# Channel blocks 4 to 7 of the normed rows in a pool of their own, 448 bytes behind the place of the weights modulo 512, in a decoder trunk on one core

## The chip, the cores and the metric

The kernel runs on one core of one Trainium2 chip. The metric is the device time of one execution in microseconds, as the median of several runs. A profile is taken of one execution apart from these.

## The reference, cut to what matters

Two layers over 512 tokens with 1024 channels, each a feed-forward part (ffn1), a mixing part (mix) and a second feed-forward part (ffn2). Everything is float32.

```python
D_MODEL, SEQ, DEPTH, D_FF = 1024, 512, 2, 2816

def swiglu(x, w_in, w_out):
    gate, up = jnp.split(x @ w_in, 2, axis=-1)
    return (jax.nn.silu(gate) * up) @ w_out

for l in range(DEPTH):
    mod = (c_act @ w_ada[l] + b_ada[l]).reshape(B, N_MOD, D_MODEL)
    sh1, sc1, gt1, sh2, sc2, gt2, sh3, sc3, gt3 = [mod[:, i, None, :] for i in range(N_MOD)]
    hn = rms_norm(h, g_ffn1[l]) * (1.0 + sc1) + sh1
    h = h + 0.5 * (1.0 + gt1) * swiglu(hn, w_ffn1_in[l], w_ffn1_out[l])
    hn = rms_norm(h, g_mix[l]) * (1.0 + sc2) + sh2
    proj = hn @ w_mix_in[l]
    ...
    mixed = jnp.concatenate([y_att, y_rwkv, y_conv], axis=-1) @ w_mix_out[l]
    h = h + (1.0 + gt2) * mixed
    hn = rms_norm(h, g_ffn2[l]) * (1.0 + sc3) + sh3
    h = h + 0.5 * (1.0 + gt3) * swiglu(hn, w_ffn2_in[l], w_ffn2_out[l])
```

## The kernel before

Activations are held transposed, 128 channels on the partitions by 512 tokens, so that the 1024 channels are eight blocks. A weight tile is 128 x 8 x 128 (4096 bytes in each partition). Each operand of a large product is kept as two tiles of a reduced-precision float type, a high part (names ending in H) and the rest (ending in L). `split` (L92 to L95) makes them: ACT casts the high part (L94), DVE subtracts it for the low one (L95). `mm3` (L86 to L91) forms a product from three matmuls: wH by xH, wH by xL and wL by xH. In a matmul the weights w are loaded (PEld in the profile) and the rows x move past them.

The tiles that the change touches come from one pool, `hnp` (L66), of 16 tiles of 128 x 512 (2048 bytes in each partition), all with one tag. `norm` (L202) takes eight pairs hnH, hnL from it, one pair for each channel block, and `apply` (L231) writes them in token halves of 256 columns: DVE forms hn_t (L235), ACT writes hnH (L236), DVE hnL (L237). `begin` (L1070) takes the first eight pairs, for the first layer. `mix` takes its results y0 to y5 and two yr through `pair` (L522), since the normed rows are done with by then; y0 to y3 are attention's four blocks, yr the recurrent part's two, y4 and y5 the convolution's.

Three users read them as moving rows:

- `projector` (L252) multiplies the eight blocks by 8 x 3 matmuls for each weight tile. Its first three tiles go in two halves of 256 columns, the others 512 wide. It does the projections of mix and the first tiles of each feed-forward part.
- `pair_in` (L378), in the feed-forward parts. It forms a block of 2 x 2 products (two halves of the channels, two halves of the tokens) with seven products instead of eight. Each product is a `prod` (L365 to L372) of 24 matmuls 256 wide. In order: ps_f from P1, ps_d from B11 (blocks 0 to 3, low half), the previous pair's last product on T4 (`flush`), ps_d from P2, ps_g from B21 (blocks 4 to 7, low half), ps_d from T3, ps_f from B22 (blocks 4 to 7, high half). P1, P2, T3 and T4 are sums of normed rows, formed once per feed-forward part. 34 pairs run in all.
- the product of w_mix_out with the y tiles, 512 wide for most tiles and 256 wide for the last.

The sums P1 to T4 are the `com` tiles. They lie in the pool of the feed-forward part behind a filling tile of GAP = 448 bytes (L300), and a second one of 64 bytes (L302) brings the tiles behind it back. In the built program the weight tiles wH and wL begin at 384 bytes modulo 512 in each partition, all hn and y tiles at 384, the act tiles (inputs of w_out) at 384, and the com tiles at 320. The last two tiles of each w_out product are 256 wide and use com's slots for their weights, so that there the weights lie at 320 and the rows at 384.

SP issues the weight loads (tile wraw; `load_w`, L243), POOL issues those of the conditioning weights (wada) and adding DMAs for the summed weights. The order on each engine is set by a scheduler when the program is built: it takes what is ready by its own model, so that another layout of the pools can change the order in which instructions stand on an engine.

Of the kernel before, what the change touches and what calls it, by code (L numbers as in the profile page):

```python
# [8 lines left out]
F32 = mybir.dt.float32  # L9
F32R = mybir.dt.float32r  # L10
# [7 lines left out]
P = 128  # L18
D = 1024
T = 512  # L20
L = 2
KD = D // P
# [10 lines left out]
GAP = 448  # L33
# [25 lines left out]
def trunk_kernel(ctx, tc, ins, out, layers=L, phases=("ffn1", "mix", "ffn2")):  # L59
# [3 lines left out]
    small_ = ctx.enter_context(tc.tile_pool(name="small", bufs=2))  # L63
    hp_ = ctx.enter_context(tc.tile_pool(name="hres", bufs=1))
    wp = ctx.enter_context(tc.tile_pool(name="wp", bufs=3))
    hnp = ctx.enter_context(tc.tile_pool(name="hnp", bufs=2 * KD))  # L66
    sp = ctx.enter_context(tc.tile_pool(name="sp", bufs=2))
    ps = ctx.enter_context(tc.tile_pool(name="ps", bufs=4, space=PSUM))
    dram = ctx.enter_context(tc.tile_pool(name="dram", bufs=1, space=bass.MemoryType.DRAM))
# [3 lines left out]
    def E(name="e", dt=F32):  # L73
        return sp.tile([P, T], dt, name=name, tag="e", bufs=4)
# [4 lines left out]
    def psum(shape, name, tag="x"):  # L79
        return ps.tile(shape, F32, name=name, tag=tag, bufs=2)  # L80
# [48 lines left out]
    def prm(l, name):  # L129
        a, b = PAR[name]  # L130
        return par[:, l, a:b]

    def cst(name):
        a, b = CON[name]
        return con[:, a:b]
# [65 lines left out]

    def norm(l, g, ish, isc, ss):  # L202

        hn = [tuple(hnp.tile([P, T], F32R, name=n, tag="hn") for n in ("hnH", "hnL")) for _ in range(KD)]
        gm = small_.tile([P, KD], F32, name="gmod", tag="gmod")
        rstd = {}

        def scale(ks=slice(0, KD)):
            stt(gm[:, ks], mod[l, isc][:, ks], 1.0, prm(l, g)[:, ks], ALU.add, ALU.mult)

        def stats(sl, sqs):

            pt = psum([P, 2], "ps_ss")
            for b in range(2):
                cols = slice(b * P, (b + 1) * P)
                parts = [ss[:, sl][:, cols]] + [sq[:, cols] for sq in sqs]
                for n, x in enumerate(parts):
                    mm(pt[:, b : b + 1], x, ones[:, :1], start=n == 0, stop=n == len(parts) - 1)
            r = E("rstd")[:, :2]
            act(r, pt, AF.Sqrt, bias=vals["eps"], scale=1.0 / D)  # L220
            nc.vector.reciprocal(r, r)
            rstd[sl.start] = r

        def spread(sl):

            r, pt = rstd[sl.start], psum([P, T // 2], "ps_rstd", "r0" if sl.start else "x")
            for b in range(2):
                mm(pt[:, b * P : (b + 1) * P], r[:, b : b + 1].to_broadcast([P, P]), cst("ident"), start=True, stop=True)
            rstd[sl.start] = pt

        def apply(sl, ks=range(KD)):  # L231
            for i in ks:
                a, b, sh = hn[i][0][:, sl], hn[i][1][:, sl], mod[l, ish][:, i : i + 1]
                t = E("hn_t")[:, : T // 2]
                stt(t, h[i][:, sl], gm[:, i : i + 1], rstd[sl.start], ALU.mult, ALU.mult)  # L235
                act(a, t, AF.Identity, bias=sh)  # L236
                stt(b, t, sh, a.bitcast(F32), ALU.add, ALU.subtract)  # L237

        return hn, scale, stats, spread, apply
# [276 lines left out]
    def mix(l, hn, ss, mp, then, ready):  # L516
# [3 lines left out]
            return mp.tile([P, w], F32, name=name, tag=name, bufs=bufs)  # L520

        def pair(name):  # L522
            return tuple(hnp.tile([P, T], F32R, name=name + n, tag="hn") for n in "HL")

        def S(q, name, shape=(P, T)):
            return mp.tile(list(shape), F32, name=f"{name}{q}", tag=f"s{q}", bufs=8)
# [28 lines left out]
        k_, r_, v_, yr = {}, {}, {}, {}  # L555
# [8 lines left out]
        def products():  # L564
# [67 lines left out]
            for q in range(2):  # L632
# [11 lines left out]
                tt(cv, pt, cv, ALU.mult)  # L644
                yc.append(cv)
            xs = [pair(f"y{k}") for k in range(6)]
            for k in (4, 5):
                split(*xs[k], yc[k - 4])
# [376 lines left out]
        for q in range(2):  # L1025
            x = pair("yr")
            split(*x, yr[q])
            xr.append(x)
# [34 lines left out]
    def normed(n, ss):  # L1063
        l, p = seq[n]
        g, im = what[p]
        return norm(l, g, im, im + 1, ss)
# [1 line left out]


    def begin(pool):  # L1070
        hn = [tuple(hnp.tile([P, T], F32R, name=n, tag="hn") for n in ("hnH", "hnL")) for _ in range(KD)]
        g1 = prm(0, "g1")
        bsh, bsc = (prm(0, "b_ada")[:, i * KD : (i + 1) * KD] for i in range(2))
        col = {n: pool.tile([P, KD], F32, name=n, tag=n) for n in ("sc", "sh", "gb", "gm0", "sh0")}
# [109 lines left out]
    with tc.tile_pool(name="first", bufs=1) as fp:  # L1184
        hn, first = begin(fp)
    ready = ()
    for n, (l, p) in enumerate(seq):
# [24 lines left out]
        hn = nxt[0] if nxt else None  # L1212
# [85 lines left out]
```

## Time and profile before

| | us |
|---|---|
| median of 3 runs | 1939.34 |
| lowest, highest | 1935.11, 1943.5 |
| profiled execution | 1942.88 |
| its span in the profile | 1940.8 |
| PE busy in the span | 1904.2 |
| DVE busy | 1402.3 |
| ACT busy | 837.2 |

In the profile's timeline a row has the start and the duration of an instruction in microseconds, the engine, the line, the operation, what it writes and reads, and its shape; idle time of the engine before it stands behind in brackets. The duration of a matmul includes the time in which it overlaps the next one, so that a stream's rate is read from one start to the next. In the rows of groups the columns behind the bar are the busy time in microseconds, the mean duration in nanoseconds, and the idle time before the group with what ended it. In the view of windows each engine has its busy time in the window and its count of instructions, then follow the granted TensorE clock (1.00 is full), the DMA engines' share and the rate. Other stages than the pairs, from that view:

```profile
326.00:372.00 46.00, 46.00 (x227) 38.99 (x226) 39.46 (x68) 16.07 (x24) 6.86 (x13) 1.00 0.76 255
```

This is the product by w_out behind the pairs of the first ffn1.

### The profile page before, as it was taken

Reading aid. Unit: us, or ns where it says so; the run is one execution under the profiler, and the core shown is the slowest. Engines: PE = TensorE matmul, PEld = TensorE weight load, DVE = VectorE, ACT = ScalarE, POOL = GpSimd, SP = SyncE. Lnnn points to the kernel's source line nnn. Section 1 sums busy time; section 2 is a strip of 40 time slices with the busy share of each in tenths; the row PEclk is TensorE's granted clock in tenths of the full one; section 3 lists DMA queues with packets and bytes.
Section 4 is the critical chain, followed back from the end, with each engine's and each line's share of the span. In section 5 each row is a group of like instructions: output and inputs, shape, how many; then the busy total and the mean of one; then the engine's idle time right before and its main releaser. Section 6 shows DMA issues by size and latency. Waiting matters only on the chain.

```text
span 1940.8 us, 33354 instructions
## 1 busy us (share of the span) xinstructions
PE 1904.2 (98%) x13664; PEld 1675.8 (86%) x13664; DVE 1402.3 (72%) x2183; ACT 837.2 (43%) x1272; POOL 130.8 (7%) x212
## 2 busy tenths in 40 slices
PE   8999999999999999999989999999999999999999
PEld 6898899886777899899889989989767788988998
DVE  6687687758976877677858776776589677773862
ACT  4443255346432554155345524543563234532541
POOL 0101100000000001110100020110000000010000
PEclk8999999999999999999999999999999999999999
DMA  7657876611211475876726678662211125664741
GB/s 295 247 163 227 255 194 188 203 68 47 63 51 61 141 198 180 275 207 190 236 73 194 171 256 240 190 218 102 87 54 58 58 74 172 182 210 133 193 132 66
DMA packets 104312, 308.23 MB, mean 159 GB/s; under 512 B 23392, under 2 KB 24416, under 8 KB 103136
## 3 DMA queue, kind: packets, MB, share of 16 engines
q1 hardware_dynamic: 75936, 203.34, 30.6%
q0 software_dynamic: 28224, 102.77, 20.6%
q8 instruction: 107, 1.75, 0.4%
q14 instruction: 45, 0.37, 0.1%
HBM read 302.66 MB, written 3.41 MB: 158 GB/s over the span
## 4 chain that ended last, share of the span: by engine, by line
PE 68%; DVE 11%; DMA 10%; issue 6%; ACT 3%; POOL 1%; SPq 0%; DVEq 0%; ACTq 0%; POOLq 0%
PE ps_mm L89 10%; PE ps_mm L90 10%; PE ps_mm L91 10%; PE ps_d L370 6%; PE ps_d L371 6%; PE ps_d L372 6%; DMA wada<-in_wadaT 4%; PE ps_f L372 3%; PE ps_f L370 3%; PE ps_f L371 3%; DVE wL L95 3%; DVE wada L152 2%; PE ps_g L372 2%; ACT wH L94 1%; PE ps_g L371 1%
## 5 line engine op out<-in xcount | busy, mean ns | idle before, releaser
L94 ACT CAST wH<-wraw 128x1024 fp32r<-128x1024 f32 (+2 forms) x292 | 267.1, 922 | 518.8 <-PE ps_mm L90 243.8
L95 DVE TENSOR_TENSOR wL<-wraw,wH 128x1024 fp32r<-128x1024 f32 (+2 forms) x292 | 307.8, 1059 | 110.6 <-ACT wH L94 108.8
L89 PE MATMUL ps_mm<-actH,wH 128*128 128x512 f32 (+1 forms) x784 | 290.1, 370 | 0.0
L91 PE MATMUL ps_mm<-actH,wL 128*128 128x512 f32 (+1 forms) x784 | 289.4, 369 | 0.4 <-DVE wL L95 0.4
L90 PE MATMUL ps_mm<-actL,wH 128*128 128x512 f32 (+1 forms) x784 | 289.3, 369 | 0.0
L89 PE MATMUL ps_mm<-hnH,wH 128*128 128x512 f32 (+1 forms) x760 | 278.2, 370 | 6.8 <-ACT hnH L94 2.9
L91 PE MATMUL ps_mm<-hnH,wL 128*128 128x512 f32 (+1 forms) x760 | 276.7, 365 | 0.5 <-DVE wL L95 0.5
L90 PE MATMUL ps_mm<-hnL,wH 128*128 128x512 f32 (+1 forms) x760 | 275.3, 363 | 0.4
L370 PE MATMUL ps_d<-comH,wH 128*128 128x256 f32 x816 | 228.4, 280 | 4.7 <-ACT s L392 4.3
L371 PE MATMUL ps_d<-comL,wH 128*128 128x256 f32 x816 | 226.6, 278 | 0.0
L372 PE MATMUL ps_d<-comH,wL 128*128 128x256 f32 x816 | 226.3, 277 | 0.0
L152 DVE SCALAR_TENSOR_TENSOR wada<-wada,crep 128x1024 f32<-128x1024 f32 x140 | 167.8, 1221 | 49.8 <-DMA wada<-in_wadaT 49.5
L95 DVE TENSOR_TENSOR wL<-sum,wH 128x1024 fp32r<-128x1024 f32 x102 | 124.9, 1225 | 69.4 <-ACT wH L94 63.9
L89 PEld LDWEIGHTS ps_mm<-hnH,wH 128*128 128x128 f32 x760 | 143.9, 191 | 35.8 <-issue 6.7
L94 ACT CAST wH<-sum 128x1024 fp32r<-128x1024 f32 x102 | 107.2, 1051 | 152.5 <-PE ps_d L371 69.5
L91 PEld LDWEIGHTS ps_mm<-actH,wL 128*128 128x128 f32 x784 | 149.0, 190 | 24.9 <-DVE wL L95 0.8
L90 PEld LDWEIGHTS ps_mm<-actL,wH 128*128 128x128 f32 x784 | 149.1, 190 | 24.2
L89 PEld LDWEIGHTS ps_mm<-actH,wH 128*128 128x128 f32 x784 | 149.0, 190 | 24.3
L91 PEld LDWEIGHTS ps_mm<-hnH,wL 128*128 128x128 f32 x760 | 144.9, 191 | 24.6 <-issue 3.2
L90 PEld LDWEIGHTS ps_mm<-hnL,wH 128*128 128x128 f32 x760 | 144.8, 191 | 23.8 <-issue 2.8
L370 PEld LDWEIGHTS ps_d<-comH,wH 128*128 128x128 f32 x816 | 154.3, 189 | 7.5 <-ACT s L392 5.5
L371 PEld LDWEIGHTS ps_d<-comL,wH 128*128 128x128 f32 x816 | 154.3, 189 | 0.0
(354 smaller groups left out, 3907.3 us busy)
## 6 DMA issues: line engine op xcount, KB each, us to landing
wada<-in_wadaT POOLq DMA_DIRECT2D x128, 512.0 KB, 4.8
wraw<-in_wmi SPq DMA_DIRECT2D x40, 512.0 KB
wraw<-in_w2p SPq DMA_DIRECT2D x36, 512.0 KB
wraw<-in_w1p SPq DMA_DIRECT2D x32, 512.0 KB
wraw<-in_w1o SPq DMA_DIRECT2D x32, 384.0 KB
wraw<-in_w2o SPq DMA_DIRECT2D x32, 384.0 KB
wraw<-in_w1i SPq DMA_DIRECT2D x20, 512.0 KB
wraw<-in_w1o SPq DMA_DIRECT2D x32, 320.0 KB
```

What stands on the lines that cost most here:

```text
L89: mm(acc, wH, xH, start=start, stop=False)
L90: mm(acc, wH, xL, start=False, stop=False)
L91: mm(acc, wL, xH, start=False, stop=stop)
L94: nc.scalar.copy(hi, src)
L95: nc.vector.tensor_sub(lo, src, hi.bitcast(F32))
L152: stt(w, w, 1.0, crep, ALU.mult, ALU.mult, accum_out=out_)
L370: mm(pt[:, i], wH, x[k][0], start=start and i + k == 0, stop=False, skip_group_check=True)
L371: mm(pt[:, i], wH, x[k][1], start=False, stop=False, skip_group_check=True)
L372: mm(pt[:, i], wL, x[k][0], start=False, stop=k == 3, skip_group_check=True)
```

## The change

The one pool of 16 tiles becomes two of eight. The first holds blocks 0 to 3 of the normed rows, and y0 to y3. The second begins behind a filling tile of 448 bytes and holds blocks 4 to 7, and y4, y5 and yr. Behind it a filling tile of 64 bytes makes the sum 512, so that everything that follows keeps its place modulo 512. In the built program the second pool's tiles begin at 320 modulo 512; the weights, the first pool, com and act stay at 384, 384, 320 and 384. The number and kind of instructions are as before.

```diff
-    hnp = ctx.enter_context(tc.tile_pool(name="hnp", bufs=2 * KD))
+
+    hnp = [ctx.enter_context(tc.tile_pool(name="hnp", bufs=KD))]
+    shift = ctx.enter_context(tc.tile_pool(name="shift", bufs=1))
+    shift.tile([P, GAP // 4], F32, name="shift")
+    hnp.append(ctx.enter_context(tc.tile_pool(name="hnp2", bufs=KD)))
+    shift = ctx.enter_context(tc.tile_pool(name="shift2", bufs=1))
+    shift.tile([P, (512 - GAP) // 4], F32, name="shift2")
...
-        hn = [tuple(hnp.tile([P, T], F32R, name=n, tag="hn") for n in ("hnH", "hnL")) for _ in range(KD)]
+        hn = [tuple(hnp[k // 4].tile([P, T], F32R, name=n, tag="hn") for n in ("hnH", "hnL")) for k in range(KD)]
...
-            return tuple(hnp.tile([P, T], F32R, name=name + n, tag="hn") for n in "HL")
+            pool = hnp[name in ("y4", "y5", "yr")]
+            return tuple(pool.tile([P, T], F32R, name=name + n, tag="hn") for n in "HL")
...
-        hn = [tuple(hnp.tile([P, T], F32R, name=n, tag="hn") for n in ("hnH", "hnL")) for _ in range(KD)]
+        hn = [tuple(hnp[k // 4].tile([P, T], F32R, name=n, tag="hn") for n in ("hnH", "hnL")) for k in range(KD)]
```

The order on the engines changes at two places of each layer. The lines of the changed kernel are six or seven higher. The first place is the end of mixing, on DVE: the low parts of the y tiles (y0L to y5L, yrL), a weight's low part wL, the convolution's sum conv_y, and TT of the recurrent part. Before:

```order
L95 TENSOR_TENSOR y4L<-conv_y,y4H 128x512
L644 TENSOR_TENSOR conv_y<-ps_mm,conv_y 128x512
L95 TENSOR_TENSOR wL<-wraw,wH 128x768
L836 TENSOR_TENSOR TT_5439<-TT_5439,ps_tt 128x512
L95 TENSOR_TENSOR y5L<-conv_y,y5H 128x512
L95 TENSOR_TENSOR y0L<-qr,y0H 128x512
L95 TENSOR_TENSOR y1L<-qr,y1H 128x512
L95 TENSOR_TENSOR y2L<-qr,y2H 128x512
L95 TENSOR_TENSOR y3L<-qr,y3H 128x512
L95 TENSOR_TENSOR yrL<-y_4882,yrH 128x512
```

And in the changed program, at the same place:

```order
L101 TENSOR_TENSOR y4L<-conv_y,y4H 128x512
L651 TENSOR_TENSOR conv_y<-ps_mm,conv_y 128x512
L101 TENSOR_TENSOR y0L<-qr,y0H 128x512
L843 TENSOR_TENSOR TT_5450<-TT_5450,ps_tt 128x512
L101 TENSOR_TENSOR y5L<-conv_y,y5H 128x512
L101 TENSOR_TENSOR y1L<-qr,y1H 128x512
L101 TENSOR_TENSOR wL<-wraw,wH 128x768
L101 TENSOR_TENSOR y2L<-qr,y2H 128x512
L101 TENSOR_TENSOR yrL<-y_4893,yrH 128x512
L101 TENSOR_TENSOR y3L<-qr,y3H 128x512
```

The weight's wL stands four rows later, y0L comes where it was, and yrL goes ahead of y3L. ACT's casts of the high parts move in the same way.

The second place is the start of ffn2, on DVE as well: the last residual h of mix, the normed rows' low parts hnL, and the low parts wL of ffn2's first weights. Before:

```order
L283 SCALAR_TENSOR_TENSOR h_96<-ps_mm,cm,h_96 128x256
L235 SCALAR_TENSOR_TENSOR hn_t<-h_96,gmod,ps_rstd 128x256
L237 SCALAR_TENSOR_TENSOR hnL<-hn_t,mod_6_3101,hnH 128x256
L95 TENSOR_TENSOR wL<-wraw,wH 128x1024
L237 SCALAR_TENSOR_TENSOR hnL<-hn_t,mod_6_3101,hnH 128x256
L95 TENSOR_TENSOR wL<-wraw,wH 128x1024
L237 SCALAR_TENSOR_TENSOR hnL<-hn_t,mod_6_3101,hnH 128x256
L221 RECIPROCAL rstd<-rstd 128x2
```

And in the changed program:

```order
L241 SCALAR_TENSOR_TENSOR hn_t<-h_107,gmod,ps_rstd 128x256
L289 SCALAR_TENSOR_TENSOR h_107<-ps_mm,cm,h_107 128x256
L243 SCALAR_TENSOR_TENSOR hnL<-hn_t,mod_6_3112,hnH 128x256
L101 TENSOR_TENSOR wL<-wraw,wH 128x1024
L243 SCALAR_TENSOR_TENSOR hnL<-hn_t,mod_6_3112,hnH 128x256
L227 RECIPROCAL rstd<-rstd 128x2
L101 TENSOR_TENSOR wL<-wraw,wH 128x1024
L243 SCALAR_TENSOR_TENSOR hnL<-hn_t,mod_6_3112,hnH 128x256
```

The residual h stands one row later, behind a row of hn_t, and the reciprocal of the second half's norm goes ahead of the second wL.

## The prediction

> **What bounds the kernel now.** I read the page from the top: the span, the busy times, the granted clock, then the chain of work that ended last.
>
> ```profile
> span 1940.8 us, 33354 instructions
> ...
> PE 1904.2 (98%) x13664; PEld 1675.8 (86%) x13664; DVE 1402.3 (72%) x2183; ACT 837.2 (43%) x1272; POOL 130.8 (7%) x212
> ...
> PEclk8999999999999999999999999999999999999999
> ...
> PE 68%; DVE 11%; DMA 10%; issue 6%; ACT 3%; POOL 1%; SPq 0%; DVEq 0%; ACTq 0%; POOLq 0%
> ```
>
> PE is busy for 1904.2 of 1940.8 us at nearly its full granted clock, and it holds 68% of the chain. Next I cut out the stretch in which the pairs of the first feed-forward part run, by the view of windows.
>
> ```profile
> core 0: us, PE busy (x) PEld busy (x) DVE busy (x) ACT busy (x) POOL busy (x), PEclk, DMA share, GB/s
> 248.00:326.00 78.00, 78.00 (x673) 78.00 (x673) 59.14 (x64) 43.25 (x58) 5.92 (x8) 1.00 0.66 191
> ```
>
> PE has no idle time at all there, the clock is 1.00, and DVE, the next busiest, needs 59.14 of 78.00 us. So in this stage the time is the number of matmuls times the time from one matmul's start to the next. The change removes no matmul. It can win only if it shortens that step. Busy PE isn't PE at its best, so I read the steps from the timeline of PE in one pair:
>
> ```profile
> 294.28 0.28 PE L370 MATMUL ps_d<-comH,wH 128*128 128x256 f32 x1
> ...
> 297.00 0.28 PE L370 MATMUL ps_g<-hnH,wH 128*128 128x256 f32 x1
> ...
> 299.86 0.28 PE L370 MATMUL ps_d<-comH,wH 128*128 128x256 f32 x1
> ...
> 302.60 0.28 PE L370 MATMUL ps_f<-hnH,wH 128*128 128x256 f32 x1
> ...
> 305.46 0.29 PE L370 MATMUL ps_f<-comH,wH 128*128 128x256 f32 x1
> ```
>
> Between two of these rows lie 24 matmuls, one product of the pair. P2 (com tiles) takes 2.72 us, B21 (hn tiles) 2.86, T3 (com) 2.74, B22 (hn) 2.86. Per matmul that is 113.3 and 119.2 ns. All are 256 wide, with the same kind of weights, no wait, at the same clock. What differs is the operand that moves: by the program's layout the com tiles begin 448 bytes behind the place of the weights modulo 512, and the hn tiles stand at the place of the weights. This is the whole effect that the change can use: it puts blocks 4 to 7 of hn, y4, y5 and yr where com stands now. That a place decides and not the kind of tile is supported by a third case, act tiles with weights that lie in com's slots, which have an offset of the other sign:
>
> ```profile
> 368.53 0.28 PE L89 MATMUL ps_mm<-actH,wH 128*128 128x256 f32 x1
> ...
> 371.71 0.28 PE L89 MATMUL ps_mm<-actH,wH 128*128 128x256 f32 x1
> ```
>
> 27 matmuls in 3.18 us are 117.8 ns, between the two.
>
> **The change part by part.** First, how many matmuls get another place. The rows are groups of one shape; behind the count stand busy time, mean ns of one, and idle time before them.
>
> ```profile
> L370 PE MATMUL ps_d<-comH,wH 128*128 128x256 f32 x816 | 228.4, 280 | 4.7 <-ACT s L392 4.3 <-ACT s L397 0.3
> L90 PE MATMUL ps_mm<-hnL,wH 128*128 128x512 f32 x520 | 207.0, 398 | 0.1
> L372 PE MATMUL ps_g<-hnH,wL 128*128 128x256 f32 x272 | 77.1, 284 | 2.7 <-DVE wL L95 2.7
> L372 PE MATMUL ps_f<-hnH,wL 128*128 128x256 f32 x272 | 76.8, 282 | 0.0
> L90 PE MATMUL ps_mm<-hnL,wH 128*128 128x256 f32 x240 | 68.2, 288 | 0.3
> L90 PE MATMUL ps_mm<-yrL,wH 128*128 128x512 f32 x24 | 9.4, 391 | 0.0
> L89 PE MATMUL ps_mm<-y4H,wH 128*128 128x512 f32 x12 | 4.9, 412 | 0.0
> L90 PE MATMUL ps_mm<-yrL,wH 128*128 128x256 f32 x16 | 4.5, 282 | 0.0
> L89 PE MATMUL ps_mm<-y4H,wH 128*128 128x256 f32 x8 | 2.3, 282 | 0.0
> ```
>
> Every such group occurs three times, for the three terms of the split product. The pairs: ps_g (B21) and ps_f (B22) have 272 x 3 = 816 each, in 34 pairs of 24. The projector's halves: 240 x 3 = 720, of which blocks 4 to 7 are 360. The y tiles 256 wide: yr 16 x 3, y4 and y5 8 x 3 each, in all 96. The 512 wide ones: hn 520 x 3 / 2 = 780, yr 72, y4 and y5 36 each, in all 924.
>
> *Pairs.* B21 and B22 go from 2.86 to 2.72 us: 0.28 per pair. A com run behind an hn run now takes 2.74 against 2.72 behind another com run, and two in each pair (T3, and the next pair's P1) follow shifted tiles then: 0.04 more. 34 x 0.32 = **-10.9 us**. PE has no idle time that could take this back in the steady pairs, and what feeds it has room: 0.32 us of some 20 (seven products of 2.72 to 2.86) shortens the time in which DVE must do its work by 1.6%, and DVE uses 59.14 / 78.00 = 76% of it.
>
> *First pair.* The 4.7 and 2.7 us of idle time in the rows above stand at the start of the pair stages, where PE waits for weights. Half of what PE gains ahead of them comes back as a longer wait: I take +1.
>
> *Other 256-wide ones.* 360 + 96 = 456 at 119.2 - 113.3 = 6 ns are 2.7 us. At the start of ffn2 PE waits for DVE and ACT (row at 634.93 below), so that some of the gain only lengthens a wait: I count **-2.0**.
>
> *512 wide.* Here the trace shows the offset nowhere: act, hn and y tiles all stand at the place of the weights. The nearest rows:
>
> ```profile
> 118.91 0.39 PE L91 MATMUL ps_mm<-hnH,wL 128*128 128x512 f32 x1
> ...
> 122.31 0.39 PE L91 MATMUL ps_mm<-hnH,wL 128*128 128x512 f32 x1
> 122.53 0.28 PE L370 MATMUL ps_f<-comH,wH 128*128 128x256 f32 x1
> ...
> 125.36 0.28 PE L370 MATMUL ps_d<-hnH,wH 128*128 128x256 f32 x1
> ```
>
> Fifteen steps in 3.40 us are 226.7 ns. Per column that is 0.443 ns, and the shifted 256-wide step, 113.3 / 256, is 0.443 too, while the aligned one is 119.2 / 256 = 0.466. Read so, the 512-wide matmul already runs at the better rate, and the offset has nothing to give it. Read per matmul, it has: from 256 to 512 columns the aligned step grows by 226.7 - 119.2 = 107.5, which leaves a fixed 11.7 ns, and if the offset takes 5.9 of it at either width, the 924 gain 5.5 us. On the other side, the last two rows show com behind 512-wide work: 24 in 2.83 us, 118 ns in place of 113.3, for the whole run; and act tiles behind com begin slower than 226.7:
>
> ```profile
> 162.21 0.39 PE L89 MATMUL ps_mm<-actH,wH 128*128 128x512 f32 x1
> ...
> 162.91 0.39 PE L89 MATMUL ps_mm<-actH,wH 128*128 128x512 f32 x1
> ```
>
> Three in 0.70 us are 233 ns. Each tile now switches place in mid-sum, twelve matmuls here and twelve there; at +4 ns for each of the 924 that costs 3.7 us. Ends -5.5 and +3.7; I take **0**, since the equal rates per column are the closest match.
>
> [...]
>
> *Writing the tiles.* ACT and DVE now write half of the hn tiles at the other place. The com tiles show its price against weights of the same shape at the other one:
>
> ```profile
> L95 DVE TENSOR_TENSOR comL<-q,comH 128x1024 fp32r<-128x1024 f32 x16 | 19.5, 1221 | 6.8 <-ACT comH L94 6.8
> L95 DVE TENSOR_TENSOR wL<-sum,wH 128x1024 fp32r<-128x1024 f32 x102 | 124.9, 1225 | 69.4 <-ACT wH L94 63.9 <-PE ps_g L372 5.2
> ```
>
> 1221 against 1225 ns: nothing. The two filling tiles are never written.
>
> *Order.* Two places per layer change order: the end of mixing, and the start of ffn2.
>
> ```profile
> 574.68 0.95 DVE L95 TENSOR_TENSOR wL<-wraw,wH 128x768 fp32r<-128x768 f32 x1
> ...
> 639.61 1.22 DVE L95 TENSOR_TENSOR wL<-wraw,wH 128x1024 fp32r<-128x1024 f32 x1
> ...
> 574.00:584.00 10.00, 10.00 (x140) 7.59 (x143) 7.09 (x12) 5.86 (x10) 0.00 (x0) 1.00 0.12 41
> 630.00:645.00 15.00, 14.52 (x114) 13.48 (x113) 12.78 (x27) 6.72 (x14) 0.00 (x0) 1.00 0.40 130
> ...
> 634.93 0.50 PE L89 MATMUL ps_mm<-hnH,wH 128*128 128x256 f32 x2 [0.16 <-ACT hnH L236]
> ```
>
> At the first, a wL of 0.95 us goes behind three y splits; the splits queued behind it on DVE come earlier, and PE's next matmuls wait for those. PE is busy 10.00 of 10.00 us there, so other matmuls cover the move; without that cover it is one wL, 0.95 us a layer. At the second, one wL of 1.22 us stands one or two rows later, and hnL rows, for which PE waits, are queued behind it or freed from it. PE idles 0.48 of 15 us. Ends: -0.48 and +1.22 a layer. Over both layers -1.0 to +4.3 in all; I take 0, the value of PE's full cover at the first place.
>
> Sum: -10.9 + 1 - 2.0 + 0 + 0 = **-12 us** (11.9). The profiled execution took 1942.88 us around its span of 1940.8, 3.5 above the median 1939.34 of the three runs; it becomes 1930.9, and the median **1927.3**.
>
> **The rivals.**
>
> *A: the 512-wide matmuls gain too.* The reading per matmul: -12 - 5.5 = -17.5, **1921.8**. For it: the fixed 11.7 ns. Against it: the equal rate per column.
>
> *B: the 512-wide matmuls lose by switching.* -12 + 3.7 = -8.3, **1931.0**. For it: 233 behind com, 118 behind 512-wide work. Against: the steps settle at 226.7 again.
>
> *C: the shifted runs in the pairs sit in the slow state.* 118 in place of 113.3 for 1632 matmuls takes 7.7 back, and with the rest about -3.5: **1935.8**. Against it: com between hn runs ran at 113.3 to 114.
>
> *D: the offset does nothing for hn.* Then something else in com is faster: **1939.3**. [...] The trace disagrees so far: 113.3 against 119.2, and 117.8 for a third offset, at the same clock without waits.
>
> *E, slower: the 512-wide matmuls on shifted tiles fall behind their weight load.* The dearest step of this width that I found is
>
> ```profile
> 578.05 0.51 PE L90 MATMUL ps_mm<-y5L,wH 128*128 128x512 f32 x1
> 578.39 0.40 PE L91 MATMUL ps_mm<-y5H,wL 128*128 128x512 f32 x1
> ```
>
> 340 ns, 113 above 226.7: here something that is hidden elsewhere wasn't. If the new place brings part of that into each of the 924, the 12.9 us of the 256-wide ones are used up at 14 ns each; at 27 ns the kernel is 12 us slower, **1951**. Against it: at half the width and the same offset the load stays hidden.
>
> **How the numbers follow.** Chances: forecast 0.40, A 0.25, B 0.20, C 0.07, D 0.03, E 0.05. About 0.5%, 9.7 us, is what a measurement of this kernel can tell from no change, so "faster" means below 1929.6. The forecast with its order term (1926 to 1931.5) lies below it for four fifths, A wholly, B for a fifth: 0.32 + 0.25 + 0.04 = 0.61. Slower is most of E, 0.04; the rest, 0.35, is within. The range goes from A with 1 us of the order's gain and 2 of the runs' scatter, 1919, to C, 1936, and leaves out D, E and the tails, some 0.15.
>
> **What would show it.** In the changed profile, 24 matmuls of ps_g and of ps_f on hn should lie 2.72 us apart: 2.86 would show D, 2.83 C. The means of the ps_g and ps_f groups fall from 284 and 282 toward 278. Twelve 512-wide steps on blocks 4 to 7 should take 226.7 ns each: 221 shows A, 231 B, over 240 E. The idle time before ps_d and ps_g shows the term of the first pair. PE idle time at the end of mixing, or over 0.5 us at the start of ffn2, shows a cost of the order. The prediction is wrong if the pairs gain and the total doesn't: then a wait outside the pairs took it, and the chain would show more DVE or DMA.

## The result, and the profile after

| | median, us | runs |
|---|---|---|
| before | 1937.64 | 6 (1933.77 to 1943.5) |
| changed | 1924.38 | 6 (1920.34 to 1927.08) |

The ratio is 0.9927, with a 95% interval of 0.9907 to 0.9947: 13.3 us less by the medians. The changed kernel was compared twice more with runs of before beside it (e4 and e9 below), which gave 0.996 [0.9943, 0.9976] and 0.9954 [0.9935, 0.9972]. So the kernel is faster by 0.4 to 0.7% as the three ratios have it, by 0.2 to 0.9% as their intervals do, and the first comparison is the largest of the three.

The first lines of the changed kernel's page, span and busy times:

```profile
span 1918.4 us, 33360 instructions
## 1 busy us (share of the span) xinstructions
PE 1889.2 (98%) x13664; PEld 1658.9 (86%) x13664; DVE 1401.7 (73%) x2183; ACT 836.8 (44%) x1272; POOL 130.7 (7%) x212
```

PE is still busy for 98% and the other engines do what they did. This profiled execution, of 1920.34 us, is the fastest of its six runs, and the one of before, of 1942.88 us, lies close to the slowest of its own six, 1943.5: 22.4 us lie between the two spans, and not all of that is the change.

The timeline of PE in one pair of the changed kernel, the first matmul of each product (start, duration, line, what it writes and reads):

```profile
293.92 0.28 PE L376 MATMUL ps_g<-hnH,wH 128*128 128x256 f32 x1
...
296.64 0.28 PE L376 MATMUL ps_d<-comH,wH 128*128 128x256 f32 x1
...
299.36 0.28 PE L376 MATMUL ps_f<-hnH,wH 128*128 128x256 f32 x1
...
302.08 0.28 PE L376 MATMUL ps_f<-comH,wH 128*128 128x256 f32 x1
...
304.80 0.28 PE L376 MATMUL ps_d<-hnH,wH 128*128 128x256 f32 x1
...
307.66 0.29 PE L376 MATMUL ps_d<-comH,wH 128*128 128x256 f32 x1
```

B21 and B22 take 2.72 us each now, as com does, and so do T3 and the next pair's P1 (2.74 before). The last two rows are B11, whose blocks 0 to 3 did not move: still 2.86. The steady pairs did what was forecast, to the hundredth of a microsecond.

The 512-wide products did not. First a whole weight tile of a projection before, 24 matmuls, with the first of each group of four blocks:

```profile
62.69 0.39 PE L89 MATMUL ps_mm<-hnH,wH 128*128 128x512 f32 x1
...
65.41 0.39 PE L89 MATMUL ps_mm<-hnH,wH 128*128 128x512 f32 x1
...
68.13 0.39 PE L89 MATMUL ps_mm<-hnH,wH 128*128 128x512 f32 x1
```

Twelve steps take 2.72 us in both halves, 226.7 ns each. The same in the changed kernel:

```profile
61.65 0.39 PE L95 MATMUL ps_mm<-hnH,wH 128*128 128x512 f32 x1
...
64.39 0.39 PE L95 MATMUL ps_mm<-hnH,wH 128*128 128x512 f32 x1
...
67.19 0.39 PE L95 MATMUL ps_mm<-hnH,wH 128*128 128x512 f32 x1
```

Blocks 0 to 3 need 2.74 us, blocks 4 to 7 2.80, that is 233.3 ns a step. The place that makes a 256-wide step shorter by 6 ns makes a 512-wide one longer by 6.6. The 20 ns that the unmoved half loses lie in its first five steps behind the switch, of 226 to 236 ns each; the seven later ones are at 226 and 227 again.

For the rest of the text I read all steps of a trace in this way: the time from one large matmul's start to the next one's, by width and place, over those without a break (under 135 ns at 256 columns, under 250 at 512). They are sorted by the addresses in the built programs, so that these means are worked out from the traces and are not rows of a view.

### The profile page after: what moved, and what is told of

It is laid out like the page before. It is cut to its first block, busy times and chain, and to the rows that moved or that the text cites. A ratio compares the mean times of both kernels' runs of the same rounds, so it can differ in the third digit from the quotient of the medians.

```text
span 1918.4 us, 33360 instructions
## 1 busy us (share of the span) xinstructions
PE 1889.2 (98%) x13664; PEld 1658.9 (86%) x13664; DVE 1401.7 (73%) x2183; ACT 836.8 (44%) x1272; POOL 130.7 (7%) x212
```

## The experiments

All compare with runs of the kernel before on the same chip.

### e1: the new order alone

The filling tile is 512 bytes, so that no tile has another place modulo 512, while every engine's order is the changed kernel's.

```diff
-    shift.tile([P, GAP // 4], F32, name="shift")
+    shift.tile([P, 512 // 4], F32, name="shift")
...
-    shift = ctx.enter_context(tc.tile_pool(name="shift2", bufs=1))
-    shift.tile([P, (512 - GAP) // 4], F32, name="shift2")
```

> Two pools of eight as in the change, but the filling tile between them is 512 bytes, so every hn and y tile stays at the place of the weights; the order on the engines is the changed kernel's. Theory P (places make the change): 256-wide hn steps stay at 119 to 120 ns, 512-wide ones at 227 to 228, and the time is that of before within 3 us. Theory O (part of the gain comes from the new order, which waits less): 5 to 7 us faster than before with the steps of before, the idle time of PE falling by as much. Theory S (what the steps do not explain is scatter of the waits from execution to execution): as P, and this profile's idle time of PE differs from that of before by some us though the places are the same.

Ratio 0.9997 [0.9984, 1.001]: the order is worth nothing that can be measured, and theory O, which needed 5 to 7 us, falls. The interval still leaves room for 3.1 us. The steps are those of before (119.3 ns at 256 wide on hn, 227.9 at 512). What differs most between this trace and that of before is a wait. In the view of waits (engine, line, releaser: us in total, times, the longest) before had, at the three places where a w_out product ends and PE forms the sum of squares ps_ss:

```profile
PE ps_ss L218 <- DVE ss L195: 6.7, 3, 3.7
```

and e1:

```profile
PE ps_ss L222 <- DVE ss L199: 3.8, 2, 2.1
```

In three traces of the changed kernel it was 2.1 us (the first), 4.7 (e4) and 6.1 (e9). Between executions of one and the same kernel this wait thus changes by up to 4.0 us, which is theory S for a part of the difference.

### e2: all eight blocks at the other place

One pool of 16 tiles behind the 448 bytes, the order of before.

```diff
+    shift = ctx.enter_context(tc.tile_pool(name="shift", bufs=1))
+    shift.tile([P, GAP // 4], F32, name="shift")
     hnp = ctx.enter_context(tc.tile_pool(name="hnp", bufs=2 * KD))
+    shift = ctx.enter_context(tc.tile_pool(name="shift2", bufs=1))
+    shift.tile([P, (512 - GAP) // 4], F32, name="shift2")
```

> All eight blocks and all y tiles stand 448 bytes behind the place of the weights; one pool, order of before. Theory P (the place sets each step: 113.4 to 114 ns at 256 wide, 233.3 at 512 wide): 3360 steps 256 wide gain 5.5 ns each, 18 us, com gains 1 more, 1848 steps 512 wide lose 5 ns each against before's mean of 228, 9.5 us: 9 to 10 us faster than before, no better than the change. Theory W (512-wide steps lose because the place switches in the middle of a sum): nothing switches here, 512-wide steps fall back to 227, and the kernel is 19 to 20 us faster than before.

Ratio 0.9992 [0.9974, 1.0009]. Both theories missed. The 512-wide steps are at 233.3 ns though nothing switches, against theory W. But the 256-wide ones, with 816 more of them at the better place in the pairs than in the change, have a mean of only 115.7 ns. The timeline of PE shows why. The last pair's product on T4 and P2 behind it are 48 steps; the first two rows bound them in the pairs ahead of the first w_out products, the last two in the pairs behind these:

```profile
146.48 0.28 PE L374 MATMUL ps_d<-comH,wH 128*128 128x256 f32 x1
...
152.13 0.28 PE L374 MATMUL ps_g<-hnH,wH 128*128 128x256 f32 x1
...
251.50 0.28 PE L374 MATMUL ps_d<-comH,wH 128*128 128x256 f32 x1
...
256.94 0.28 PE L374 MATMUL ps_g<-hnH,wH 128*128 128x256 f32 x1
```

48 steps in 5.65 us are 117.7 ns, in 5.44 us 113.3. The same operands at the same places run at two levels. The upper one held from 130.7 to 240 us in this trace, through 288 512-wide steps of w_out, and ended behind a break of PE at 240.43 (0.30 us to the next start). In the change the upper level ends, in each pair, with the product B11 on the unmoved blocks: behind it the steps stood at 113.3 again, and in 83 of the 102 pairs of the change's three traces they stay there until the next B11 or the end of the stage. In the other 19, each the first pair of a stage, the upper level comes back behind a break of PE, of 0.33 us or more in all but one. That the four blocks that stay are what keeps the change's other products fast is the nearest reading, but it is argued and not shown: e8 below moves all eight too, and the hn steps of its pairs have a mean of 113.8 ns. The runs of e2 spread over 15.5 us, so that one trace may not stand for all of them. In this trace moving all eight gave the gain back, and the sums of its steps agree with the time: against e1, hn at 256 wide -11.3 us, com +4.5, y at 256 wide -0.7, 512 wide +8.1, in all +0.6.

### e3: the act tiles at the other place

```diff
-            ap_.tile([P, (512 - GAP) // 4], F32, name="gap2", tag="gap2")
```

> Kernel before with the second filling tile behind com left out, so that the act tiles, 1872 moving operands 512 wide, stand 448 bytes behind the place of the weights in unbroken streams; the last 480 at 256 wide then stand at the place of their weights. Theory P: act steps 512 wide go from 226.7 to 233.3 ns, 12.4 us, and the 256-wide ones from 117.7 to 119.3, 0.8 us: 13 us slower than before. Theory W (only switching costs): 226.7 still, 1 us slower at most. Rival A of the prediction (512-wide gain): 221, 11 us faster.

The steps came as theory P has them: 233.3 ns over all 1872 (and 119.7 for the 480 at 256 wide), 13.2 us in sum. Two rows of its timeline bound 48 of the 512-wide ones, from a product's first:

```profile
161.78 0.39 PE L89 MATMUL ps_mm<-actH,wH 128*128 128x512 f32 x1
...
172.97 0.39 PE L89 MATMUL ps_mm<-actH,wH 128*128 128x512 f32 x1
```

11.19 us, 233.1 ns. In unbroken streams of one place the loss is there from end to end, so that it belongs to the place and not to the switching; rival A falls as well.

The 256-wide rows of this run also tell the distance from the place itself. They now begin at 320 modulo 512, where com's rows run at 113.3 ns, but their weights begin at 320 too. These two rows bound 48 steps:

```profile
369.09 0.28 PE L89 MATMUL ps_mm<-actH,wH 128*128 128x256 f32 x1
...
374.83 0.28 PE L89 MATMUL ps_mm<-actH,wH 128*128 128x256 f32 x1
```

5.74 us, 119.6 ns: the step of aligned rows. So it is the distance between rows and weights that counts, and not the place of the rows alone.

The time moved less than the steps: 1.0027 [1.0013, 1.0041], 5 us. The wait at the end of the w_out products took up a part of the rest:

```profile
PE ps_ss L218 <- DVE ss L195: 0.2, 1, 0.2
```

0.2 us where before had 6.7 and e1 3.8. With PE slower in this stage, DVE is no longer late at its end. The ends of the w_out products thus gave back 3.6 to 6.5 us of the 13.2. The granted clock gave back another part. In the view of windows, 15 us around the second of these ends, before and then e3 (the clock is the third figure from the end):

```profile
975.00:990.00 15.00, 10.77 (x77) 10.48 (x77) 9.74 (x18) 6.99 (x12) 0.00 (x0) 0.89 0.10 35
...
975.00:990.00 15.00, 14.27 (x119) 13.98 (x118) 10.40 (x25) 6.01 (x13) 0.00 (x0) 1.00 0.11 35
```

In before the clock stood at half for 3.4 us there (0.50 from 983.0 to 986.4), behind a wait of 3.7 us, and a 256-wide step took some 0.21 us. Over the nine runs of e3 the mean granted clock is 0.9952, over the 32 of before beside it 0.9939; of 1935 us that is some 2.5 (an estimate). With the wait it makes 6 to 9 us, and 8 are needed.

### e4 and e9: the change twice more

No edit.

> The changed kernel once more, for a second trace and more times. Steps worked out from the first two traces: 256-wide hn -11.0 us, com -1.3, y -0.3, 512-wide hn and y +5.8, in sum -7 us; the times said -13. Theory S: this trace has the same steps but another sum of waits, by up to 5 us, and the ratio comes nearer to 0.996. Theory O or another lasting gain in the waits: ratio 0.993 again, and PE's waits as short as in the first trace of the change.

> The changed kernel a third time, for a third trace and times on another day's share of the chip. By the steps of its first two traces against e1 (same order, places of before): 256-wide hn -10, 512-wide hn and y +5.4, com and the rest under 1, in sum -5 to -6 us. Theory S (the rest of what the first comparison showed is scatter of waits): 0.995 to 0.998. Theory V (some lasting saving of waits besides the steps): 0.992 to 0.994, and waits of PE at the ends of the w_out products shorter than in e1.

0.996 [0.9943, 0.9976] and 0.9954 [0.9935, 0.9972], both in the range that S gave. In these two traces more products in the first pair of a stage, behind its waits, sit at the upper level (117.8) than in the first trace, so that the pairs gained 8.2 us in both, against 10.4 in the first. The waits on ss were 4.7 and 6.1 us, against 2.1:

```profile
PE ps_ss L224 <- DVE ss L201: 2.1, 2, 1.3
```

is the row of the first trace of the change, and of e9:

```profile
PE ps_ss L224 <- DVE ss L201: 6.1, 3, 3.2
```

The granted clock differs with them, here around the second of these waits, in the first trace and in e9:

```profile
968.00:983.00 15.00, 14.48 (x121) 14.17 (x121) 9.34 (x25) 5.86 (x13) 0.00 (x0) 1.00 0.11 35
...
975.00:990.00 15.00, 13.87 (x94) 13.79 (x95) 8.92 (x23) 5.59 (x12) 0.00 (x0) 0.77 0.10 35
```

Over the whole spans it is 0.996 in the first trace, 0.992 in e4 and 0.991 in e9, and 0.993 in those of before and e1. By that the first trace lost up to 8.7 us less to the clock than those of e4 and e9, 0.0045 of 1930 (an estimate), with the same program.

### e5, e6, e7, e10, e11, e12: other places

Only the two filling tiles differ, with s bytes in the first and 512 - s in the second; in e7 the act tiles lie 64 bytes behind the place of their 512-wide products' weights as well, by a second filling tile of 128 bytes behind com.

```diff
-    shift.tile([P, GAP // 4], F32, name="shift")
+    shift.tile([P, s // 4], F32, name="shift")
...
-    shift.tile([P, (512 - GAP) // 4], F32, name="shift2")
+    shift.tile([P, (512 - s) // 4], F32, name="shift2")
```

> The changed kernel with a first filling tile of 64 bytes in place of 448: blocks 4 to 7, y4, y5 and yr begin 64 bytes behind the place of the weights modulo 512 instead of 448. Theory P2 (each distance has its own step, no rule known yet; the nearest row is act's last tiles, 64 bytes behind their weights): 117.8 ns at 256 wide, 3 us gained over 2080 steps in place of the change's 11; at 512 wide open, 227 if only the distance of 448 disturbs, 233 if every distance does (5 us lost). Time: 0 to 3 us slower or faster than before, 5 to 8 slower than the change.

> As e5, with 256 bytes in both filling tiles: the farthest place from the weights modulo 512. Theory P2 leaves this open: if the loss at 512 wide belongs to any distance, 233 ns; if it belongs to a small one, 227 or less. If the gain at 256 wide grows with distance, under 113.3; if it is bound to 448, 119.

> Filling tiles of 384 and 128 bytes, so that hn's second half lies 384 bytes behind (128 ahead of) the place of the weights, and act tiles 64 bytes behind it through a second filling tile of 128 bytes behind com. Looked at for the steps, not for the time. If the two-sided picture of e3 (448: 233.3 at 512 wide) is one of sign, act at 64 behind stays at 226.7 or less; if of any distance, 233. For hn at 384: 256-wide between 113.3 and 119.

> The changed kernel with filling tiles of 480 and 32 bytes: the second half lies 32 bytes ahead of the place of the weights, between the places 0 (119.3 and 226.7 ns at 256 and 512 wide) and 64 ahead (113.3 and 233.3). Theory M (a place inside a 64-byte step acts as the place that it begins in, or as a mean): 256-wide 113.3 to 119, 512-wide 226.7 to 233, time between before and the change. If a place has both the low step at 256 wide and 226.7 at 512 wide, this or e12 would be it, and the kernel would be 10 us faster than before.

> Filling tiles of 416 and 96 bytes: 96 ahead of the weights, between 64 ahead (113.3, 233.3) and 128 ahead (118.8, 232.4). Theory M: 113 to 119 and 232 to 233 ns. Looked at for the steps.

> Filling tiles of 32 and 480 bytes: 32 behind the weights, between 0 (119.3, 226.7) and 64 behind (117.8, 230.5). Theory M: 118 to 119 and 227 to 230 ns. Looked at for the steps.

Mean steps in ns on hn tiles that begin so many bytes behind the place of the weights, from the traces as said above:

| bytes behind | 256 wide | 512 wide | kernel, ratio |
|---|---|---|---|
| 0 | 119.3 | 227.9 | e1, 0.9997 |
| 32 | 117.0 | 233.3 | e12, one run |
| 64 | 117.8 | 230.5 | e5, 0.9987 [0.997, 1.0003] |
| 256 | 119.3 | 227.8 | e6, one run |
| 384 | 118.8 | 232.4 | e7, one run |
| 416 | 117.5 | 233.7 | e11, one run |
| 448 | 113.8 to 114.1 | 233.3 | the change |
| 480 | 118.1 | 233.3 | e10, 1.0003 [0.999, 1.0016] |

The single runs of e6, e7, e11 and e12 took 1935.06, 1935.22, 1933.86 and 1935.65 us, within the spread of before. A tile at 256 has the steps of one at 0, 119.3 and 227.8 ns against 119.3 and 227.9. The timeline of e6, a whole projection tile with its moved half between the last two rows:

```profile
62.28 0.39 PE L95 MATMUL ps_mm<-hnH,wH 128*128 128x512 f32 x1
...
65.00 0.39 PE L95 MATMUL ps_mm<-hnH,wH 128*128 128x512 f32 x1
...
67.72 0.39 PE L95 MATMUL ps_mm<-hnH,wH 128*128 128x512 f32 x1
```

2.72 and 2.72 us, as before. This is the only pair of places 256 bytes apart that was run. Every other place tried makes a 512-wide step longer, by 2.6 to 5.8 ns. All of them make a 256-wide one shorter, but only 448 by more than 2.4 ns. e5 came as theory P2 had it at 256 wide, and at 512 wide between the two values that it left open. e7's act tiles at 64 took 228.9 ns at 512 wide, which neither of the two values named for them was. Theory M failed at e12 (117.0 and 233.3 against 118 to 119 and 227 to 230) and by under 1 ns at the 512-wide steps of e10 and e11; there is no place with both low steps among those tried.

### e8: two halves in place of 512 columns

e2, with each 512-wide product of normed rows done as two of 256 columns.

```diff
+    def mm3h(acc, w, k, x, start, stop):
+        for n, s in enumerate(HALVES):
+            mm3(acc[:, s], w, k, x, s, start and n == 0, stop and n == 1)
...
-                mm3(pt, w, k, hn[k], ALL, k == 0, k == KD - 1)
+                mm3h(pt, w, k, hn[k], k == 0, k == KD - 1)
...
-                mm3(pts[n], ws[n], k, hn[k], ALL, k == 0, k == KD - 1)
+                mm3h(pts[n], ws[n], k, hn[k], k == 0, k == KD - 1)
```

> All eight blocks at 448 as in e2, and each 512-wide product of normed rows done as two of 256 columns (1560 more matmuls and weight loads). In e2 the 256-wide steps had two levels, 113.3 and 117.8 ns, each kept over hundreds of steps and left only at a wait. Theory L (the level is drawn at each wait or change of width): if the stages without 512-wide work fall on 113.3, two halves take 226.7 in place of e2's 233.3, 9 us gained over e2 and about 8 over before; if they fall on 117.8, two halves take 235.6, and the kernel is 2 to 4 us slower than e2. Rival (the upper level needs 512-wide neighbours): always 113.3 in mix.

Ratio 0.9983 [0.996, 1.0006]. The hn steps have a mean of 114.9 ns, and both levels occur in mix, each for some tens of steps at a time: that is a mixture of theory L's two cases. The rival falls: between 403 and 437 us the level changes several times, at breaks of PE, with no 512-wide matmul in the stretch. It does not beat the change, whose three ratios lie between 0.9927 and 0.996. At the means of its unbroken steps, the large matmuls of this trace sum to 12.9 us less than those of e1, but its span is only 2.9 shorter. In mix PE waits on DVE for T, Sc and k instead: the rows ps_x 2.7, ps_pt 2.2, ps_mm 2.0 and ps_sc 2.0 us of its view of waits sum to 8.9, against 0.5 in e1.

## Why the prediction was right, and where not

The time of the first comparison, 1924.38, lies 2.9 us under the forecast, with the forecast's sign; over the three comparisons the mean ratio 0.9947 is 10.3 us less than before, against a forecast of 12. But the sum came out near for reasons that are only partly those given, and that the first comparison came so close is luck: its steps explain about half of it, and e4's interval, at most 0.57% less, does not reach the forecast's 0.62%. By its steps:

- **Pairs, -10.9 us.** Right. Against e1, the steps of the pairs gave -10.4 in the first trace and -8.2 in e4 and e9. The difference is the upper level in the first pairs of a stage, rival C, which occurs for a few products and not for all.
- **First pair, +1.** Not seen: PE's wait for ACT's s tile at ps_d was 4.3 us before and 3.9 to 4.5 after, that for DVE's wL at ps_g 2.7 before but 0.6 in e1 already.
- **Other 256-wide ones, -2.0.** Right: 4.9 ns on 360 projector steps, with some 0.3 from the y tiles: -2.0.
- **512 wide, taken as 0.** This is the step that failed, a term put at nothing where the runs show a cost. The shifted steps take 233.3 ns in place of 226.7, and the unmoved ones behind a switch lose 1.6 on average: hn +4.9 us and y +0.4, 5.3 in sum, outside the bound of +3.7. The reading "equal rate per column" was wrong, and so was the reading per matmul, rival A. Rival B had the sign and most of the size, by the wrong reason: the loss is the place's own (e3), and the switching adds only 20 ns to a tile.
- **Writing the tiles, 0.** Borne out: DVE's and ACT's busy times are 1401.7 and 836.8 us against 1402.3 and 837.2.
- **Order, 0.** Borne out by e1, within the 3.1 us that its interval leaves.
- **Rival D**, that the place does not matter, is refuted: e1 and the change differ in nothing but the place, and the moved blocks' steps in the pairs took 113.4 to 113.8 ns in the change's first trace, against a mean of 119.3 on hn in e1. Over all runs, steps of 113.3 to 119.3 and 226.7 to 233.7 ns show that the places of rows and weights matter to each other. By what mechanism they do, no run here shows.
- **Rival E** had the sign for 512 wide, at a quarter of the 27 ns that it needed.

The steps alone give -10.4 - 2.0 + 5.3 = -7 us in the first trace and -5 in the others. The times gave -14.1, -7.7 and -8.9 (the three ratios on their medians of before, 1937.64, 1936.72 and 1936.79). Some of what is left is scatter of the waits, above all of that on ss, which was 6.7 us in the trace of before and 3.8 in e1, and some is the granted clock, whose mean over the runs of the change was 0.9947 in the first comparison, 0.9942 in e4 and 0.9935 in e9; 0.001 of it is some 1.9 us (an estimate). Against e1, with the same order and beside it, e4's median is 5.6 us less (1928.82 against 1934.38), about what the steps give. What they do not explain in e4 thus lies between before and e1. Whether a lasting saving of 3 to 4 us hides in it, the runs do not settle: the three intervals reach from 0.9907 to 0.9976, and the wait on ss alone spread by 4.0 us between traces of one kernel.

## What to carry to other kernels

When a trace shows that the same matmul steps differ by a few nanoseconds with the place of its rows, the place is worth a try, but its value has to be measured at each width that the tiles are used at: here one place gained 6 ns at 256 columns and lost 6.6 at 512. A rate that agrees by division (0.443 ns per column at both widths) is no evidence for the width that was not measured. Where a sum of small terms comes out right, compare each term's steps over several traces before believing the sum: one trace's waits here moved by more than the terms.

## What the runs showed of the hardware that was not expected

- The step of a stream of matmuls here differed with how its rows and its weights lie to each other in a partition: 113.3 to 119.3 ns at 256 columns, 226.7 to 233.7 at 512. The places 0 and 256, the only two 256 bytes apart, gave the same steps (119.3 and 227.9 against 119.3 and 227.8).
- The best place tried at one width was among the worst at the other: 448 behind gave 113.3 at 256 columns and 233.3 at 512, where the places ran from 226.7 to 233.7.
- At 448 behind, 256-wide steps have two levels, 113.3 and 117.8 ns, each held for hundreds of steps, across other widths. A product of aligned rows brought the lower one back in every pair of the change, but e8 shows the lower one through most of the pairs without such rows. What sets the level stays open.
- In the trace of before the granted clock stood at half for 3.4 us behind each of the three waits on ss, of 2.1, 3.7 and 0.9 us; in e3, whose longest such wait was 0.2, it stayed at 1.00 there. Behind the wait of 3.7 us a 256-wide step took some 0.21 us in place of 0.12, so that this wait cost more than its length. Not every wait did: in e7, with three such waits of 0.9 to 1.5 us, the clock stayed at 1.00, and in the trace of before it stayed at 1.00 behind one of 1.2 us on ACT's s tile, which ended at 236.80.
